# Passages between stages in program order with early products, and triangle matrices on ScalarE

## The chip, the cores and the metric

The kernel runs on one core of one Trainium2 chip. The core has TensorE for matrix products, VectorE, ScalarE and GpSimd for work on elements, each with a queue of its own that is worked off in order, and DMA queues for transfers (all weights come over SyncE's). Engines wait for one another by semaphores. The metric is the device time of one execution in microseconds (us); a value is the median of several runs.

## The reference

256 tokens with 1024 features pass through one network in float32. A root-mean-square norm stands in front of each part, and each part's result is added to `x`:

```
x = x + mixer(norm(x))            # window attention and gated linear attention
x = x + (silu(conv(h@Wa)) * (h@Wu)) @ Wo     with h = norm(x)     # FFN, causal conv over 3 tokens
x = x + pool_mixer(norm(x))       # causal means over 2, 4, 8, 16 tokens, then one product per group
x = x + (silu(h@Wg) * (h@Wu)) @ Wd           with h = norm(x)     # dense FFN
x = x + ssd(norm(x))              # state-space mixer, 32 heads of 64 in 8 groups, chunks of 128 tokens
x = x + top-2 of 8 experts(norm(x))
norm(x) = x / sqrt(mean(x*x) + 1e-6) * gain
```

In the state-space mixer each head has a decay `dtA` per token. Within a chunk the weight of token s in token l is exp of the sum of `dtA` over the tokens between them, for s up to l, times the inner product of two projected vectors; the result takes that matrix times the inputs, plus the state carried over from the chunk before.

## The kernel before

**Tiling.** The 256 tokens are two tiles of 128, t = 0 and 1. A row of 1024 features is two halves of 512, c = 0 and 1. Each float32 operand of a product is held as a high and a low part, and a product is done three times (high by high, high by low, low by high): `mm3`, L337 to L341, or, with the tokens as the moving side, one product of 2x256 columns and one of 256 (`sums`, L761, L770 and L771).

**Weights.** A piece is 1 MB, 128x2048. SyncE's queue fetches it into a ring of raw pieces; `piece` (L294) then splits it in two halves of 1024 columns: ScalarE copies the high part (`wh`, L391), VectorE subtracts it to get the low part (`wl`, L392). `wh` and `wl` have a ring of six halves each, so a seventh copy waits until TensorE is through with the first.

**A norm and its passage.** `norm_tile` (L368) squares the two halves on ScalarE (L373, with a sum per token), multiplies the second half by the gain on GpSimd (L374), and VectorE adds the two sums (L376) and makes the inverse root in eight small steps (`rsqrt`: `rs_x` L354, `rs_y` L358, then `rs_t` L361 and `rs_y` L365 three times). Then VectorE scales the first half (L378) and ScalarE the second (L379) into `xn`. `turn` transposes `xn` on TensorE (L404) and splits the result into `xT`, again a copy on ScalarE and a subtraction on VectorE. `Turned.tile` (L60) does this for one tile. For the FFN and the dense FFN it puts 11 dummy products (`keep_warm`, L62) in front of the second tile's transposes, and sets gates: the low part of the next weight piece is made by GpSimd, and the three pieces behind it are split only after the last `xT` split.

**What comes before a passage.** The mixer ends with `w_out` (two chunks of 512 columns, each with two pieces held, first tile 0, then tile 1), the FFNs with `down`: three pieces held, 36 products for tile 0 and then 36 for tile 1. `PoolMixer.tile` (L82) stands between the FFN and the dense FFN: its means are products with a band matrix (L99, and L101 for the first tile's tokens or the second's), then one product per group and `add_x` (L431).

**The state-space mixer.** `ssd` (L838) interleaves by a list of steps: `x0` to `x7` project and convolve a chunk of channels (products L756 to L758 into `acc`, convolution L802 and L805, gating L935 and L936), `z` chunks project the gate, and `c0` to `c7` are the cores, one for each group of four heads. A core makes, for each tile and for the high and low part of `dtA`, four triangle matrices side by side (`ua`, 128x512, L972): the upper triangle of ones times the decay of its row, on GpSimd. TensorE sums them (L974), ScalarE takes exp (`w`, L976), VectorE multiplies by the inner products (L977), and TensorE applies the result (L982). GpSimd also scales the inputs (`xd`, `xe`, `xs`, L952 to L955).

**What sets the order.** A list scheduler that runs the program in a model of the chip puts each engine's instructions in order. `in_order(begin)` (L1464) pins the order in which those since `begin` were written, on TensorE, VectorE and ScalarE, among themselves; instructions written later can still be put between them.

## Time and profile before

| | us |
|---|---|
| median of 3 runs | 1767.45 (1766.4 to 1769.3) |
| profiled execution | 1770.0 |
| its span | 1768.2 |

| engine | busy us | share of the span |
|---|---|---|
| TensorE (PE) | 1721.1 | 97% |
| VectorE (DVE) | 1495.5 | 85% |
| ScalarE (ACT) | 1245.7 | 70% |
| GpSimd (POOL) | 154.0 | 9% |

The stages follow one another: the mixer to 251, the FFN from 259 to 444, the pool mixer, the dense FFN from 465 to 649, the state-space mixer to 880, the router, and the experts from some 905 to 1740. A matmul's record is longer than the distance to the next, so TensorE's share of 97% is not a share of its peak; how dense the products are is read from the distances of their starts. Idle time of an engine counts only where another waits for it.

### The profile page before, as it was taken

How to read it: one execution, taken by the hardware profiler on the slowest of the kernel's cores; microseconds unless marked ns; L12 is line 12 of the kernel's file. 1: busy time of each engine (PE TensorE's matmuls, PEld its weight loads, DVE VectorE, ACT ScalarE, POOL GpSimd, SP SyncE). 2: the span in 40 equal slices, each digit the busy share in tenths (PEclk: the TensorE clock that was granted, in tenths of full speed). 3: DMA queues.
4: the chain of work that ended last, by engine and by line, in shares of the span. 5: the costliest groups of instructions: out<-in, count | busy, mean ns of one | idle time of the engine just before them, and what ended most of it. 6: DMA issues, size and time to landing. Idle time of an engine off the chain costs nothing.

```text
span 1768.2 us, 23830 instructions
## 1 busy us (share of the span) xinstructions
PE 1721.1 (97%) x8731; PEld 1420.7 (80%) x8731; DVE 1495.5 (85%) x1652; ACT 1245.7 (70%) x1412; POOL 154.0 (9%) x118
## 2 busy tenths in 40 slices
PE   8999989999999999999999999999999999999996
PEld 6878878888788879998878777777777787777775
DVE  7477668777766659997779999999999999999997
ACT  5564446655655546555468898888889888988895
POOL 1034010001100012572000000000000000000000
PEclk9999999999999999999989999999999999999999
DMA  8433455555455545425659999999999999999993
GB/s 288 167 120 123 143 183 211 185 188 188 143 188 188 188 150 204 143 97 179 253 187 373 420 421 421 420 418 420 405 402 420 421 420 415 421 420 410 421 420 157
DMA packets 72719, 501.31 MB, mean 284 GB/s; under 512 B 8322, under 2 KB 9346, under 8 KB 14355
## 3 DMA queue, kind: packets, MB, share of 16 engines
q1 hardware_dynamic: 72594, 499.71, 72.7%
q8 instruction: 71, 1.16, 0.3%
q14 instruction: 54, 0.43, 0.1%
HBM read 498.63 MB, written 1.05 MB: 283 GB/s over the span
## 4 chain that ended last, share of the span: by engine, by line
PE 55%; DVE 32%; issue 9%; ACT 2%; POOL 1%; DMA 0%; DVEq 0%; SPq 0%; ACTq 0%
DVE wl L313 23%; PE acc L339 7%; PE acc L340 7%; PE acc L341 7%; PE pr L770 5%; PE tp L770 5%; PE tp L771 2%; PE pr L771 2%; PE pr L339 2%; PE pr L340 2%; PE pr L341 2%; PE pr L1219 1%; PE pr L1218 1%; PE acc L516 1%; DVE wl L392 1%
## 5 line engine op out<-in xcount | busy, mean ns | idle before, releaser
L313 DVE TENSOR_TENSOR wl<-raw,wh 128x2048 fp32r<-128x2048 f32 x330 | 736.7, 2280 | 0.0
L311 ACT ACTIVATE wh<-raw 128x2048 fp32r<-128x2048 f32 x330 | 620.9, 1913 | 70.2 <-PE pr L341 38.8
L392 DVE TENSOR_TENSOR wl<-raw,wh 128x1024 fp32r<-128x1024 f32 (+2 forms) x248 | 308.2, 1255 | 112.7 <-ACT wh L391 109.8
L391 ACT ACTIVATE wh<-raw 128x1024 fp32r<-128x1024 f32 (+3 forms) x254 | 259.3, 1036 | 90.0 <-PE acc L341 60.1
L1219 PE MATMUL pr<-wl,xg 128*128 128x512 f32 x560 | 221.9, 396 | 5.5 <-DVE wl L313 5.5
L1218 PE MATMUL pr<-wh,xg 128*128 128x512 f32 x560 | 224.2, 400 | 0.0
L340 PE MATMUL pr<-wl,xg 128*128 128x512 f32 x336 | 135.8, 404 | 1.5 <-DVE wl L1462 1.5
L339 PE MATMUL pr<-wh,xg 128*128 128x512 f32 x336 | 136.6, 407 | 0.0
L341 PE MATMUL pr<-wh,xg 128*128 128x512 f32 x336 | 134.1, 399 | 0.0
L1219 PEld LDWEIGHTS pr<-wl,xg 128*128 128x128 f32 x560 | 105.3, 188 | 33.9 <-DVE wl L313 12.5
L770 PE MATMUL pr<-xT,wh 128*128 128x512 f32 x352 | 125.0, 398 | 2.0 <-DVE xT L392 2.0
L770 PE MATMUL tp<-xT,wh 128*128 128x512 f32 x352 | 124.9, 398 | 0.0
L1218 PEld LDWEIGHTS pr<-wh,xg 128*128 128x128 f32 x560 | 105.3, 188 | 22.2
L1219 PE MATMUL acc<-wl,hT 128*128 128x512 f32 x280 | 113.3, 405 | 1.6 <-DVE wl L313 0.4
L1218 PE MATMUL acc<-wh,hT 128*128 128x512 f32 x280 | 111.1, 397 | 0.7 <-DVE hT L392 0.7
L339 PE MATMUL acc<-wh,xT 128*128 128x512 f32 (+3 forms) x256 | 99.2, 389 | 1.6 <-ACT xT L391 0.9
L340 PE MATMUL acc<-wl,xT 128*128 128x512 f32 (+3 forms) x256 | 98.8, 387 | 0.0
L771 PE MATMUL tp<-xT,wl 128*128 128x256 f32 x352 | 98.6, 280 | 0.0
L771 PE MATMUL pr<-xT,wl 128*128 128x256 f32 x352 | 98.6, 280 | 0.0
L341 PE MATMUL acc<-wh,xT 128*128 128x512 f32 (+3 forms) x256 | 98.5, 387 | 0.1
L1536 POOL TENSOR_TENSOR raw<-x,raw 128x512 f32<-128x512 f32 x2 | 2.5, 1276 | 936.4 <-DVE x L431 936.4
L770 PEld LDWEIGHTS pr<-xT,wh 128*128 128x128 f32 x352 | 66.1, 188 | 18.4 <-DVE xT L392 2.4
(389 smaller groups left out, 3472.6 us busy)
## 6 DMA issues: line engine op xcount, KB each, us to landing
raw<-in_w_eg SPq DMA_DIRECT2D x110, 1024.0 KB, 10.6
raw<-in_w_ed SPq DMA_DIRECT2D x110, 1024.0 KB, 10.6
raw<-in_w_eu SPq DMA_DIRECT2D x110, 1024.0 KB, 10.8
raw<-in_w_ffn_in SPq DMA_DIRECT2D x22, 1024.0 KB, 4.9
raw<-in_w_dense_in SPq DMA_DIRECT2D x22, 1024.0 KB, 4.9
raw<-in_w_xbc SPq DMA_DIRECT2D x16, 1024.0 KB, 4.8
raw<-in_w_ffn_out SPq DMA_DIRECT2D x11, 1024.0 KB, 5.0
raw<-in_w_dense_out SPq DMA_DIRECT2D x11, 1024.0 KB, 4.9
```

The costliest lines, as they stand in the source:

```text
L311: self.nc.scalar.activation(ab[0], raw, AF.Copy)
L313: lambda: v.tensor_tensor(ab[1], raw, ab[0].bitcast(F32), op=OP.subtract)
L339: mm(ps, st[0], mv[0], start=start, stop=False)
L340: mm(ps, st[0], mv[1], start=False, stop=False)
L341: self.last_mm = mm(ps, st[1], mv[0], start=False, stop=stop)
L391: a = nc.scalar.activation(h, src, AF.Copy)
L392: b = v.tensor_tensor(l, src, h.bitcast(F32), op=OP.subtract)
L516: nc.tensor.matmul(ps[:, m], wt.cut(a, k * 256 + m * P, P), xT[b][:, k], start=(k == 0 and a == 0 and b == 0), stop=(k == KB - 1 and b == 1))
L770: nc.tensor.matmul(ps, wh, xT[2][:, k], start=k == 0, stop=False)
L771: nc.tensor.matmul(ps[:, 0], wl, xT[0][:, k], start=False, stop=k == KB - 1)
L1218: self.nc.tensor.matmul(ps, st, mv[0], start=start, stop=False)
L1219: self.nc.tensor.matmul(ps, st, mv[1], start=False, stop=stop)
```

## The change

**Norms.** `Normed` takes the place of `norm_tile`: `half(t, c)` squares one half as soon as its sum is there, with the factor 1/(2*1024) inside the square, and VectorE multiplies the first half by the gain; `scale(t)` makes the root in one VectorE step fewer (`rsqrt_of`), ScalarE scales the first half and VectorE makes the second. The dummy products of the passages and the gates are gone.

**Early piece.** `Lead` fetches and splits the first weight piece of the next stage during the passage, outside `piece`. `LeadSums` makes its products for one tile and half of the piece at a time: 8 products of 256 columns and 8 of 128, four times, so 64 products in place of 32 of 512 and 256 columns. `LeadRows` does the same for the mixer's first gate chunk (416 columns, four halves of 832).

**Program order.** `gemm_nat(then=)`, `down_last`, `ready`, `rest` and `both` write the passages out step by step, and `in_order` pins them.

**Triangle matrices.** Each `ua` is made by four ScalarE copies of 128x128 with a scale per partition, 128 in all, in place of one GpSimd product.

```diff
+    def half(self, t, c):
+        net, nc, xn = self.net, self.net.nc, self.xn
+        h = slice(c * 512, (c + 1) * 512)
+        nc.scalar.activation(xn[:, t, 512:], net.x[:, t, h], AF.Square, scale=(0.5 / D) ** 0.5,
+                             accum_out=self.ss[t][:, c:c + 1])
+        if c == 0:
+            nc.vector.tensor_tensor(xn[:, t, h], net.x[:, t, h], self.g[:, h], op=OP.mult)
+
+    def scale(self, t):
+        net, nc, xn = self.net, self.net.nc, self.xn
+        r = net.rsqrt_of(self.ss[t], 1e-6)
+        nc.scalar.activation(xn[:, t, :512], xn[:, t, :512], AF.Copy, scale=r)
+        nc.vector.scalar_tensor_tensor(xn[:, t, 512:], net.x[:, t, 512:], r, self.g[:, 512:], op0=OP.mult, op1=OP.mult)
...
+    def rest(self):
+
+        lead, n = self.lead, self.lead.n
+        lead.subtract(n // 2)
+        self.scale(1)
+        for u in range(n // 2 + 1, n):
+            lead.subtract(u)
+        for u in range(n // 2 + 1):
+            lead.products(0, u, self.xT)
+        self.turn(1)
+        for u in range(n // 2 + 1, n):
+            lead.products(0, u, self.xT)
+        for u in range(n):
+            lead.products(1, u, self.xT)
+
+    def both(self):
+
+        ps = [self.group(0, g) for g in range(2)]
+        self.group(0, 0, ps[0])
+        net, s = self.net, slice(0, P)
+        net.nc.scalar.activation(self.xT[0][:, 4:, s], ps[1], AF.Copy)
+        self.scale(1)
+        self.early = net.nc.vector.tensor_tensor(self.xT[1][:, 4:, s], ps[1], self.xT[0][:, 4:, s].bitcast(F32), op=OP.subtract),
+        self.lead.products(0, 0, self.xT)
+        self.turn(1)
+        self.lead.products(0, 1, self.xT)
+        for h in range(2):
+            self.lead.products(1, h, self.xT)
+
...
+    def fetch(self):
+        raws = [self.net.fetch(ap, self.w) for ap in self.aps]
+        w = self.w // 2
+        self.raw = [raw[:, h * w:(h + 1) * w] for raw in raws for h in range(2)]
+        self.n, self.high, self.low = len(self.raw), {}, {}
+
+    def copy(self, u):
+        self.high[u] = self.net.whp.tile([P, 1024], F32R, name="wh")[:, :self.w // 2]
+        self.net.nc.scalar.activation(self.high[u], self.raw[u], AF.Copy)
...
+    def products(self, t, h, xT):
+        net, mm = self.net, self.net.nc.tensor.matmul
+        if (t, h) == (0, 0):
+            self.ps = [net.pr((P, 2, T)) for _ in range(2)]
+        s = slice(t * P, (t + 1) * P)
+        for k in range(4 * h, 4 * h + 4):
+            for m in range(2):
+                c = slice(k % 4 * 256 + m * P, k % 4 * 256 + (m + 1) * P)
+                mm(self.ps[m][:, :, s], self.high[h][:, c], xT[2][:, k, :, s], start=k == 0, stop=False,
+                   skip_group_check=True)
+                mm(self.ps[m][:, 0, s], self.low[h][:, c], xT[0][:, k, s], start=False, stop=k == KB - 1,
+                   skip_group_check=True)
...
+    def rest(self):
+        net, N = self.net, self.N
+        N.lead.subtract(1)
+        self.scale(1)
+        out = self.mix(0)
+        ps = self.banks()
+        self.means(1, 0, ps)
+        for c in range(2):
+            net.add_x(0, c, out[c])
+            N.half(0, c)
+        self.means(1, 1, ps)
+        self.split(1, ps)
+        N.scale(0)
+        out = self.mix(1)
+        for c in range(2):
+            net.add_x(1, c, out[c])
+            N.half(1, c)
+        N.both()
+        self.ctx.close()
...
-            gate = self.gates.pop(0) if self.gates else ()
-            if None in gate:
-                v = self.nc.gpsimd
-            for ins in gate:
-                if ins is not None:
-                    st.enter_context(self.tc.issue_after(ins.ins))
-            fine = fine or self.wide is None or len(gate) > 0
+            fine = fine or self.wide is None
...
+    def rsqrt_of(self, ss, eps):
+
+        v = self.nc.vector
+        z = self.small.tile([P, 1], F32, name="rs_x")
+        t = self.small.tile([P, 1], F32, name="rs_t")
+        y = self.small.tile([P, 1], F32, name="rs_y")
+        v.tensor_scalar(z, ss[:, 0:1], ss[:, 1:2], 0.5 * eps, op0=OP.add, op1=OP.add)
+        v.tensor_scalar(y.bitcast(I32), z.bitcast(I32), -0.5, float(0x5F3759DF - 0x400000 - 0x80000000), op0=OP.mult, op1=OP.add)
+        for _ in range(3):
+            v.tensor_scalar(t, y, y, z, op0=OP.mult, op1=OP.mult)
+            v.scalar_tensor_tensor(y, t, -1.5, y, op0=OP.add, op1=OP.mult)
+        return y
...
+            if then is not None and p == np_ - hold:
+                then.fetch()
+                for h in range(2):
+                    then.lead.copy(h)
+                    then.lead.subtract(h)
...
             def end(t, c, ps):
+                if (t, c) == (0, 1):
+                    self.start = len(nc.cur_bb.bb.instructions)
                 self.add_x(t, c, ps)
-                if c:
-                    N.tile(t)
-
-            for c in range(2):
-                self.gemm_nat(mT, I["w_out"][c], KB, end, c, last=True)
+                N.half(t, c)
+                if (t, c) == (0, 1):
+                    N.scale(0)
+
+            self.gemm_nat(mT, I["w_out"][0], KB, end, 0, last=True)
+            self.gemm_nat(mT, I["w_out"][1], KB, end, 1, last=True, then=N)
+            N.both()
+            self.in_order(self.start)
...
+        begin = len(self.nc.cur_bb.bb.instructions)
+        for c in range(2):
+            self.add_x(0, c, accs[0][c])
+            N.half(0, c)
+        N.scale(0)
+        for c in range(2):
+            for j in range(len(aps)):
+                if (c, j) == (1, 1):
+                    N.ready()
+                sums(1, c, j)
+            self.add_x(1, c, accs[1][c])
+            N.half(1, c)
+        N.rest()
+        self.in_order(begin)
...
-            z_chunk(0)
+            for t in range(2):
+                gate_z(t, 0, N.lead.ps[t][:, :416])
...
                         ua = wk.tile([P, 4, P], F32R, name="ua")
-                        nc.gpsimd.tensor_tensor(ua, self.upper[:, None, :].to_broadcast([P, 4, P]),
-                                                bc(da[:, t, hs].bitcast(F32), P), op=OP.mult)
+                        for r in range(4):
+                            nc.scalar.activation(ua[:, r], self.upper, AF.Copy,
+                                                 scale=da[:, t, 4 * g + r:4 * g + r + 1].bitcast(F32))
                         nc.tensor.matmul(ps, laterr, ua, start=j == 0, stop=j == 1)
```

Three places show what the change does to the order. The first is VectorE around the first tile's norm in front of the FFN; `rs_x`, `rs_y`, `rs_t` are the steps of the inverse root, `wl<-raw,wh` the low half of a weight piece. Before:

```order
L376 TENSOR_TENSOR ss_2109<-ss 128x1
L354 TENSOR_SCALAR rs_x<-ss_2109 128x1
L358 TENSOR_SCALAR rs_y<-rs_x 128x1
L361 TENSOR_SCALAR rs_t<-rs_y,rs_x 128x1
L365 SCALAR_TENSOR_TENSOR rs_y<-rs_t,rs_y 128x1
L361 TENSOR_SCALAR rs_t<-rs_y,rs_x 128x1
L365 SCALAR_TENSOR_TENSOR rs_y<-rs_t,rs_y 128x1
L361 TENSOR_SCALAR rs_t<-rs_y,rs_x 128x1
L365 SCALAR_TENSOR_TENSOR rs_y<-rs_t,rs_y 128x1
L378 SCALAR_TENSOR_TENSOR xn<-x,rs_y,gbc 128x512
L431 TENSOR_TENSOR x<-x,acc 128x512
```
VectorE at the same place now:

```order
L527 TENSOR_SCALAR rs_y<-rs_x 128x1
L529 TENSOR_SCALAR rs_t<-rs_y,rs_x 128x1
L530 SCALAR_TENSOR_TENSOR rs_y<-rs_t,rs_y 128x1
L544 TENSOR_TENSOR wl<-raw,wh 128x1024
L529 TENSOR_SCALAR rs_t<-rs_y,rs_x 128x1
L544 TENSOR_TENSOR wl<-raw,wh 128x1024
L530 SCALAR_TENSOR_TENSOR rs_y<-rs_t,rs_y 128x1
L544 TENSOR_TENSOR wl<-raw,wh 128x1024
L529 TENSOR_SCALAR rs_t<-rs_y,rs_x 128x1
L544 TENSOR_TENSOR wl<-raw,wh 128x1024
L530 SCALAR_TENSOR_TENSOR rs_y<-rs_t,rs_y 128x1
L69 SCALAR_TENSOR_TENSOR xn<-x,rs_y,gbc 128x512
```
Four subtractions of weights, of the second and third piece of the FFN (L544; those of the early piece have L153), now stand between the steps of one root.

The second is ScalarE in the pool mixer's passage, from the second tile's first square to its scaling (`xn,ss<-x` is a square, `xn<-xn,rs_y` the scaling, `pT<-tp` the means). Before:

```order
L373 ACTIVATE xn,ss<-x 128x512
L379 ACTIVATE xn<-xn,rs_y 128x512
L391 ACTIVATE wh<-raw 128x1024
L373 ACTIVATE xn,ss<-x 128x512
L391 ACTIVATE pT<-tp 128x4x128 x2
L373 ACTIVATE xn,ss<-x 128x512
L379 ACTIVATE xn<-xn,rs_y 128x512
```
ScalarE at the same place now:

```order
L60 ACTIVATE xn,ss<-x 128x512
L543 ACTIVATE pT<-tp 128x4x128 x2
L149 ACTIVATE wh<-raw 128x1024 x2
L543 ACTIVATE wh<-raw 128x1024 x4
L60 ACTIVATE xn,ss<-x 128x512
L68 ACTIVATE xn<-xn,rs_y 128x512
```
Six copies of weights stand between the means' copies and the second tile's last square, four of them of the pieces behind the early one; before it was one copy, further ahead.

The third is ScalarE in the state-space mixer, from one `w` to the next but one (`cv`, `xbc` belong to the convolution, `wh` to weights, `Bn` to the core). Before:

```order
L976 ACTIVATE w<-tp 128x512
L391 ACTIVATE wh<-raw 128x1024
L935 ACTIVATE xbc_6515<-cv 128x256
L802 ACTIVATE cv<-acc,cols 128x256
L391 ACTIVATE wh<-raw 128x1024
L802 ACTIVATE cv<-acc,cols 128x256
L976 ACTIVATE w<-tp 128x512
```
ScalarE at the same place now:

```order
L1170 ACTIVATE w<-tp 128x512
L1166 ACTIVATE ua<-tri,dtAl 128x128 x4
L1156 ACTIVATE Bn<-tp 128x128
L543 ACTIVATE wh<-raw 128x1024
L1128 ACTIVATE xbc_6480<-cv 128x256
L543 ACTIVATE wh<-raw 128x1024
L1128 ACTIVATE xbc_6547<-cv 128x256
L1166 ACTIVATE ua<-tri,dtAh 128x128 x4
L1170 ACTIVATE w<-tp 128x512
```
Each row `ua` with x4 is four new copies; they stand between the convolutions, the exponentials and the weight splits.

## Rows read from the trace of the kernel before

**Rows 1.** TensorE's timeline, first passage: start us, us, engine line op out<-in xcount [idle<-releaser]

```profile
251.31 1.03 PE L404 MATMUL tp<-ident,xn 128*128 128x128 f32 x8
253.32 2.79 PE L335 MATMUL tp<-xT 128*128 128x512 f32 x11 [0.98 <-DVE xT L392]
...
258.90 0.50 PE L770 MATMUL pr<-xT,wh 128*128 128x512 f32 x1 [0.98 <-DVE xT L392]
...
264.65 0.40 PE L770 MATMUL tp<-xT,wh 128*128 128x512 f32 x1
```

**Rows 2.** TensorE's timeline, third passage

```profile
654.79 1.90 PE L404 MATMUL tp<-ident,xn 128*128 128x128 f32 x8 [2.18 <-DVE xn L378]
```

**Rows 3.** Windows: stretch, its us, then each engine's busy us (instructions), granted clock, DMA

```profile
core 0: us, PE busy (x) PEld busy (x) DVE busy (x) ACT busy (x) POOL busy (x), PEclk, DMA share, GB/s
654.80:658.20 3.40, 3.40 (x13) 2.91 (x14) 1.45 (x3) 2.08 (x4) 0.00 (x0) 0.51 0.07 14
690.00:760.00 70.00, 68.48 (x542) 65.97 (x541) 69.25 (x113) 40.86 (x78) 41.76 (x39) 1.00 0.37 126
760.00:850.00 90.00, 89.28 (x546) 81.06 (x545) 72.52 (x107) 49.33 (x88) 37.20 (x33) 1.00 0.50 179
```

**Rows 4.** The chain that ended last, mixer stage: start us, us, what

```profile
753.06 5.45 POOL ua L972 x4
```

**Rows 5.** VectorE's timeline in the mixer stage

```profile
694.86 1.26 DVE L936 SCALAR_TENSOR_TENSOR xbc<-xbc,cv 128x256 f32<-128x256 f32 x1
...
702.50 0.41 DVE L936 SCALAR_TENSOR_TENSOR xbc<-xbc,cv 128x256 f32<-128x256 f32 x1
```

**Rows 6.** Groups of VectorE, 690 to 850: xcount, busy us, mean ns, idle before

```profile
L936 DVE SCALAR_TENSOR_TENSOR xbc<-xbc,cv 128x256 f32<-128x256 f32 x27 | 18.1, 673 | 2.7 <-ACT xbc L935 2.7
```

**Rows 7.** ScalarE's timeline, first passage

```profile
246.85 0.63 ACT L373 ACTIVATE xn<-x 128x512 f32<-128x512 f32 x1 [4.04 <-DVE x L431]
...
250.13 0.72 ACT L379 ACTIVATE xn<-xn,rs_y 128x512 f32<-128x512 f32 x1 [2.55 <-DVE rs_y L365]
...
258.50 3.90 ACT L391 ACTIVATE wh<-raw 128x1024 fp32r<-128x1024 f32 x4
```

**Rows 8.** VectorE's timeline, first passage

```profile
248.18 0.15 DVE L354 TENSOR_SCALAR rs_x<-ss 128x1 f32<-128x1 f32 x1
...
250.07 0.75 DVE L378 SCALAR_TENSOR_TENSOR xn<-x,rs_y,gbc 128x512 f32<-128x512 f32 x1
...
259.59 3.50 DVE L392 TENSOR_TENSOR wl<-raw,wh 128x1024 fp32r<-128x1024 f32 x3
```

**Rows 9.** TensorE's timeline, second passage

```profile
447.53 0.28 PE L339 MATMUL pr<-wh,pT 128*128 128x256 f32 x1
447.65 0.28 PE L340 MATMUL pr<-wl,pT 128*128 128x256 f32 x1
...
470.26 0.39 PE L770 MATMUL tp<-xT,wh 128*128 128x512 f32 x1
```

**Rows 10.** VectorE's timeline, second passage

```profile
443.80 0.69 DVE L431 TENSOR_TENSOR x<-x,acc 128x512 f32<-128x512 f32 x1 [2.54 <-PE acc L341]
...
449.91 0.75 DVE L378 SCALAR_TENSOR_TENSOR xn<-x,rs_y,g 128x512 f32<-128x512 f32 x1
```

**Rows 11.** Groups of GpSimd, 660 to 880

```profile
L972 POOL TENSOR_TENSOR ua<-tri,dtAl 128x512 fp32r<-128x512 f32 x16 | 24.5, 1529 | 0.6 <-PE tp L974 0.4 <-DVE dtAl L392 0.2
L972 POOL TENSOR_TENSOR ua<-tri,dtAh 128x512 fp32r<-128x512 f32 x16 | 22.2, 1389 | 23.9 <-issue 19.1 <-PE tp L974 4.8
```

**Rows 12.** Groups of ScalarE, 690 to 850

```profile
L976 ACT ACTIVATE w<-tp 128x512 f32<-128x512 f32 x16 | 9.5, 592 | 7.5 <-PE tp L974 7.5
...
L963 ACT ACTIVATE Bn<-tp 128x128 f32<-128x128 f32 x8 | 2.2, 270 | 1.8 <-PE tp L960 1.8
```

**Rows 13.** Groups of TensorE, 690 to 760

```profile
L756 PE MATMUL acc<-xT,wh 128*128 128x256 f32 x136 | 39.3, 289 | 0.0
...
L974 PE MATMUL tp<-ua,laterr 128*128 128x512 f32 x18 | 7.1, 441 | 0.8 <-POOL ua L972 0.8
```

More of the change, by code (lines that the diff above doesn't have):

```diff
@@ new lines, with __init__, group, turn @@
+class Turned(Normed):
+    def __init__(self, net, gname, lead=None):
+        super().__init__(net, net.gain(gname), net.norm.tile([P, 2, D], F32, name="xn"))
+        self.xT, self.lead = net.pair(KB), lead and lead(net)
+    def fetch(self):
+        self.lead.fetch()
+    def group(self, t, g, turned=None):
+        net, nc = self.net, self.net.nc
+        s = slice(t * P, (t + 1) * P)
+        if turned is None:
+            turned = net.tp((P, 4, P))
+            for i in range(4):
+                nc.tensor.transpose(turned[:, i], self.xn[:, t, (4 * g + i) * P:(4 * g + i + 1) * P], net.ident)
+            return turned
+        last = net.split(turned, *[x[:, 4 * g:4 * g + 4, s] for x in self.xT[:2]])
+        if t == 0:
+            self.early = last
+    def turn(self, t):
+        for g in range(2):
+            self.group(t, g, self.group(t, g))
+    def ready(self):
+        self.turn(0)
+        self.lead.ready()
+    def rest(self):
[23 more added lines that the diff above has]
+            self.lead.products(1, h, self.xT)
@@ new lines, with products @@
+class LeadRows(Lead):
+    def products(self, t, u, xT):
+        net, w = self.net, self.w // 4
+        if u == 0:
+            if t == 0:
+                self.ps = []
+            self.ps.append(net.acc())
+        s = slice(t * P, (t + 1) * P)
+        for i in range(2):
+            k, c = 2 * u + i, slice(i * w, (i + 1) * w)
+            net.mm3(self.ps[t][:, :w], (xT[0][:, k, s], xT[1][:, k, s]), (self.high[u][:, c], self.low[u][:, c]),
+                    k == 0, k == KB - 1)
+class PoolMixer(Normed):
@@ L73, in __init__ @@
     def __init__(self, net, then):
[L74 removed]
+        self.then, self.N = then, None
         I = net.I
@@ L832, in ffn @@
             N = then()
-            self.down([w_out[i + j] for j in range(3)], hs[2 * i:], accs, False, self.add_x, then=N)
+            self.down_last([w_out[i + j] for j in range(3)], hs[2 * i:], accs, N)
         return N
```

144 lines of the change are left out of this document (78 added, 66 removed).

## The prediction

> **What bounds the kernel now.** I first read the time by stretch, then, at the places the change touches, the timeline of TensorE and behind it those of VectorE and ScalarE, and last the chain that ended last. Two kinds of place are touched. At the passages between stages TensorE stands and waits for a normalized row: before the FFN it fills part of the wait with 11 dummy matmuls, 253.32 to 256.11, and only at 258.90 does the first weight piece start; the second starts at 264.65 [rows 1]. Before the state-space mixer it waits 2.18 us, for VectorE [rows 2]. In the mixer TensorE is busy, but VectorE is at its limit too: 69.25 of 70 us from 690 to 760, and 72.52 of 90 after it, with ScalarE at 40.86 and 49.33 and GpSimd at 41.76 and 37.20 [rows 3]. There GpSimd's triangle matrices hold the chain too, 5.45 us on end for four of them at 753 [rows 4], and VectorE's operations with two inputs in SBUF are stretched while GpSimd runs: the gating of `xbc` takes 1.26 us at 694.86, with a triangle matrix beside it, and 0.41 at 702.50 [rows 5]; its mean over 27 is 0.673 [rows 6]. What lies behind the mixer and its router's norm is unchanged.
>
> The sum is made against the profiled execution of 1770.0 us (span 1768.2, and 1.8 around it), which lies 2.55 above the median of 1767.45; I carry the sum of differences over to the median.
>
> **First passage, mixer to FFN.** The order of the changed kernel decides it: between the steps of the first tile's inverse root, VectorE has the four subtractions of weight pieces 1 and 2 of the FFN. Each waits for ScalarE's high copy, and that for a free half in the ring of six. The ring is full by then (four halves of `w_out`, two of the early piece), so the copies follow the halves of `w_out` as the second tile's last products give them free; the last is free where the transposes start before, 251.3 [rows 1]. From there a copy, 0.98 (3.90 for four [rows 7]), a subtraction, 1.17 (3.50 for three [rows 8]), the last root step and the product with the gain, 0.16 and 0.75, and some 0.4 between engines: the first tile's row is ready at 254.9 to 255.2, where before it was ready at 250.8 (250.07 + 0.75 [rows 8]). The second tile's sum and square (0.6 and 0.8) stand before the copies of the transposed row, so the first copy and subtraction end at 257.9. The early products of half a piece for one tile are 16; their prices are 0.12 for 256 columns (447.53 to 447.65 [rows 9]) and about 0.11 for 128 (eight transposes in 1.03 [rows 1]), so 1.84 a group, and 7.36 for four groups against 5.75 for the piece whole (258.90 to 264.65 [rows 1]). The first group fits in the wait. The second tile's root chain (1.89 from 248.18 to 250.07, and 0.75 [rows 8]) ends at 260.3, its transposes at 261.4, and three groups at 266.9. Against 264.65 that is **+2.2 us**. Without the subtractions inside the chain all of it would lie 4 us earlier and be limited by the second tile's own sum at 251.3: some 263.9, or -0.7.
>
> **Second passage, FFN to pool mixer to dense FFN.** Here four copies stand on ScalarE before the second tile's last square, and four subtractions on VectorE before its root. Its last sum was started at 443.80 [rows 10]; eight mean products (0.9) now stand before it, 444.8. The two copies of the early piece end at 445.0, the four others at 448.9, the four subtractions at 451.7, root and product at 454.2 (1.89 + 0.75 from rows 8). Before, that row was ready at 450.66 (449.91 + 0.75 [rows 10]): 3.5 later. From there I walk the order: second half of the means 455.1; the copies of the means behind the square of the new sum, 456.7; first split 458.05; 24 products 460.95; transposes of the dense FFN's first tile 462.15; their copies behind both squares of the second tile, split 464.9; one early group; the second tile's row at 467.25, transposed 468.35; three early groups to 473.85. The second dense piece started at 470.26 [rows 9]: **+3.6 us**, and 0 if the row kept its old time.
>
> **Third passage, dense FFN to the state-space mixer.** Four copies of 832 and two of 1024 columns stand before the second tile's last square. Its row comes at 657.1 where its transposes started at 654.79 before [rows 2]; 18 of the first tile's 24 products are done in the wait. Two more weight splits stand before the second tile's own. I get **+1.2 us**, bounds -0.5 and +2.
>
> **The clock.** The dummies go and TensorE now stands still for 3.7 us in the first passage and 5.5 and 3 in the second. Where it waited 2.18 us before, it came back at a granted clock of 0.51 from 654.8 to 658.2 [rows 2, 3], the lower of the two levels, and its eight transposes took 1.90 where eight at the full clock took 1.03 [rows 1, 2]. In the first passage such a stretch, from 255.2 on, falls mostly into the wait for the second tile. In the second it would fall on the 24 products. Bounds 0 and +4; I take **+1.0**, near the lower end, since most of such stretches are covered by waits that remain.
>
> **The first norm** gets a product with the gain on VectorE inside the chain in place of GpSimd's: bounds 0 and +1.5, I take **+0.5** since TensorE waits for weights right after. **The router** has one VectorE step less in each of two chains: **-0.3**.
>
> **The triangle matrices.** GpSimd loses 16 of 1.529 and 16 of 1.389 us, 46.7 in all [rows 11]; ScalarE gets 128 of 128x128 with a scale per partition. The trace has no such row. A copy with a scale per partition takes 0.72 for 512 columns [rows 7]; 512 against 128 columns is 0.592 against 0.270 [rows 12], so 0.40 for one, and about 0.1 of that overlaps the next (a copy of 1024 is 0.98 of pitch): 0.30, 38 us in all. From the 0.270 row itself it would be 0.17 and 22 us. I take 0.30, the row with the same kind of scale. The Trainium skill ("ScalarE: Activation LUTs", What ACT_TABLE_LOAD costs) gives 186 ns plus 0.833 ns per column, 93 ns more for a pointer operand and 93 ns of overlap between neighbours: an estimate of 0.293 us, 37.5 in all. It speaks against the change, and agrees with the upper row.
>
> ScalarE then has 18 matrices in the first stretch (one for each product of 512 columns [rows 13]), 72 operations or 21.6 us, on top of 40.86: 62 of 70, in a queue that also feeds every weight split and convolution. VectorE gets time back: 27 gatings of 0.673 against 0.41 are 7 us by themselves, over the stage [rows 6], and GpSimd keeps about 2/5 of its work there. The Trainium skill ("SBUF — State Buffer", SBUF: two separate sides) states the reason as a lock: a VectorE operation with two SBUF inputs and a GpSimd operation exclude each other for the whole instruction. The pair of rows 5 agrees, 0.41 against 1.26; by that rule alone the relief would be the larger end of what follows. TensorE's own gaps bound the gain: in 690 to 760 its 542 products [rows 3] (three lines of 136 with 256 columns at 0.12, 18 with 512 [rows 13] at 0.23, the other 116 at 0.11) fill 66 of 70 us, so 4, and about as much again behind 760, where GpSimd still holds the chain [rows 4] and so few rows speak that I take the same: at most -9, as an estimate. On the other side, a ScalarE that is 90% full in order could cost as much as it gives, up to +4. The row nearest is ScalarE's load with its new work, 62 of 70: I take **-3.5**.
>
> **Sum**: 2.2 + 3.6 + 1.2 + 1.0 + 0.5 - 0.3 - 3.5 = +4.7, so 1774.7 for an execution like the profiled one, and 1772 for the median.
>
> **Rivals.**
> - *Mixer relief whole* (15%): ScalarE's queue keeps up, TensorE runs at its pitches: -9 in place of -3.5, 1766.7. For it: VectorE at 69.25 of 70. Against: ScalarE at 62 of 70.
> - *The splits ahead come early* (17%): ring halves and weights are there before the root chain reaches them, and the passages cost -0.5 in all, with 0.5 of clock: 1767.45 - 0.5 + 0.5 + 0.5 - 0.3 - 3.5 = 1764.1. Against it: the six halves are all held until the last products.
> - *Both* (8%): 1758.6. This is the one clearly faster.
> - *ScalarE's queue decides in the mixer* (10%): from the point at which a triangle operation takes more than 0.35 us (18 x 4 x 0.35 + 40.86 = 66 of 70), the products of the mixer wait for ScalarE and the weight splits queue behind it: +4 in place of -3.5, 1779.7.
> - *It does not do what it says* (5%): the passages' waits come out the same as before, 1767.
>
> The forecast has 45%, with its own range 1768 to 1777. About 0.2%, 3.5 us, is what a measurement of this kernel can tell from no change. Faster than 1763.9: both, half of the early splits, and the tails of the forecast and the relief, 0.23. Slower than 1771.0: most of the forecast, ScalarE's queue, 0.44. Within: 0.33. The range leaves out most of "both" and half of ScalarE's queue: 1760 to 1779.
>
> **What would show it.** In the changed profile: the first FFN piece after the early one starts 16 us after the last `w_out` product (13.5 before), and VectorE's subtractions stand between two root steps; TensorE's wait before the second half of the means is 5 us and more; GpSimd's share falls from 9% to about 6%; the gating of `xbc` has a mean near 0.5; ScalarE passes 60 of 70 in the mixer's first stretch. I am wrong if the triangle operations take 0.2 us or less, if the high copies are done before the root chain starts, or if the half clock falls on the products of the passages.

## Result and profile after

| | before | after |
|---|---|---|
| median of 4 runs, us | 1768.38 (1766.4 to 1769.4) | 1778.58 (1778.18 to 1778.85) |
| profiled execution, us | 1770.0 | 1778.49 |
| its span, us | 1768.2 | 1776.7 |

Before has one run more here than above. The changed kernel is slower by 10.2 us: ratio 1.0058, 95% interval 1.0046 to 1.007. The prediction had the direction, but a loss of less than half that size (1772). Its forecast's own range, 1768 to 1777, does not hold the time; the wider range, 1760 to 1779, does, by 0.4 us.

The first part of the page of after: the span, then each engine's busy us, its share and its instructions.

```profile
span 1776.7 us, 23967 instructions
PE 1721.1 (97%) x8773; PEld 1426.6 (80%) x8773; DVE 1488.0 (84%) x1656; ACT 1280.4 (72%) x1540; POOL 74.5 (4%) x70
```

TensorE is as busy as before to the tenth, and the kernel is 8.5 us longer: by shares of the whole span nothing has happened. So I cut both traces into stretches, each between the starts of two named instructions: the first `x` addition after `w_out`, after the FFN's `down` and after the dense FFN's `down`; the first `cv` of the state-space mixer; the first transpose of the router's norm; the first addition of the experts.

| stretch | before, us | after | forecast |
|---|---|---|---|
| start to the end of the first mixer | 235.19 | +1.33 | +0.5 |
| first passage and FFN | 200.23 | +3.16 | +2.2 and a part of the clock's +1.0 |
| second passage, pool mixer and dense FFN | 204.83 | +6.26 | +3.6 and a part of it |
| third passage | 30.12 | +2.26 | +1.2 and a part of it |
| state-space mixer | 204.40 | -3.95 | -3.5 |
| router and first experts | 229.01 | -0.91 | -0.3 |
| rest | 664.46 | +0.33 | 0 |

The three passages together lose 11.7 us where 8.0 were forecast. The seven terms sum to the 8.5 us by which the profiled executions differ; the medians differ by 1.7 us more, and which stretch holds that the two traces don't say. How far one execution can be trusted shows in the kernels below whose code in a stretch is the same: their first passages differ by up to 0.05 us, the second by 0.9, the third by 0.5, and the start by 3.6 (a part of that is a matter of the clock, see the first norm below).

**First passage.** VectorE's timeline of after, from a step of the first tile's root to its product with the gain:

```profile
251.03 0.27 DVE L529 TENSOR_SCALAR rs_t<-rs_y,rs_x 128x1 f32<-128x1 f32 x1
251.21 1.23 DVE L544 TENSOR_TENSOR wl<-raw,wh 128x1024 fp32r<-128x1024 f32 x1
252.35 0.15 DVE L530 SCALAR_TENSOR_TENSOR rs_y<-rs_t,rs_y 128x1 f32<-128x1 f32 x1
252.62 1.23 DVE L544 TENSOR_TENSOR wl<-raw,wh 128x1024 fp32r<-128x1024 f32 x1
253.76 0.27 DVE L529 TENSOR_SCALAR rs_t<-rs_y,rs_x 128x1 f32<-128x1 f32 x1
253.98 1.23 DVE L544 TENSOR_TENSOR wl<-raw,wh 128x1024 fp32r<-128x1024 f32 x1
255.12 0.15 DVE L530 SCALAR_TENSOR_TENSOR rs_y<-rs_t,rs_y 128x1 f32<-128x1 f32 x1
255.31 0.75 DVE L69 SCALAR_TENSOR_TENSOR xn<-x,rs_y,gbc 128x512 f32<-128x512 f32 x1
```

Root steps of 0.15 to 0.27 us stand apart by a subtraction of 1.23 each, and each subtraction waits for its copy. ScalarE's timeline of after shows what the copies wait for (in brackets the idle time before, and the releaser):

```profile
250.11 1.06 ACT L543 ACTIVATE wh<-raw 128x1024 fp32r<-128x1024 f32 x1 [0.26 <-PE acc L493]
251.52 1.06 ACT L543 ACTIVATE wh<-raw 128x1024 fp32r<-128x1024 f32 x1 [0.34 <-PE acc L493]
252.89 1.06 ACT L543 ACTIVATE wh<-raw 128x1024 fp32r<-128x1024 f32 x1 [0.31 <-PE acc L493]
```

It is `acc L493`, the second tile's last products of `w_out`, as forecast: the ring of six halves is full, and the first tile's root waits for the second tile's products, which it has nothing to do with. TensorE's timeline of after:

```profile
252.41 0.39 PE L493 MATMUL acc<-wh,xT 128*128 128x512 f32 x1
256.09 1.65 PE L90 MATMUL tp<-ident,xn 128*128 128x128 f32 x8 [3.29 <-ACT xn L68]
258.74 0.58 PE L175 MATMUL pr<-xT,wh 128*128 128x256 f32 x1 [1.00 <-DVE xT L544]
...
262.22 1.58 PE L90 MATMUL tp<-ident,xn 128*128 128x128 f32 x8
263.55 0.36 PE L175 MATMUL pr<-xT,wh 128*128 128x256 f32 x1
...
269.13 0.45 PE L932 MATMUL tp<-xT,wh 128*128 128x512 f32 x1
```

TensorE starts the first tile's transposes 3.7 us after the start of its last product; before, the two followed one another [rows 1]. The first early group, 16 products, takes 3.48 us (258.74 to 262.22), the other three 5.58 together (263.55 to 269.13), so 1.86 each.

**Second passage.** ScalarE's timeline of after, then VectorE's, in front of the second tile's row:

```profile
448.07 2.00 ACT L149 ACTIVATE wh<-raw 128x1024 fp32r<-128x1024 f32 x2
449.97 3.88 ACT L543 ACTIVATE wh<-raw 128x1024 fp32r<-128x1024 f32 x4
453.76 0.62 ACT L60 ACTIVATE xn<-x 128x512 f32<-128x512 f32 x1
```

```profile
452.08 4.62 DVE L544 TENSOR_TENSOR wl<-raw,wh 128x1024 fp32r<-128x1024 f32 x4
456.62 0.20 DVE L526 TENSOR_SCALAR rs_x<-ss 128x1 f32<-128x1 f32 x1
...
458.56 0.75 DVE L69 SCALAR_TENSOR_TENSOR xn<-x,rs_y,g 128x512 f32<-128x512 f32 x1
```

The sum that the square at 453.76 needs had been there since 451.1 (started at 450.34); the six copies stood ahead of it, and the four subtractions ahead of the root. TensorE, in the same passage of after, then waits 4.38 us:

```profile
459.34 3.78 PE L227 MATMUL tp<-band,xn 128*128 128x128 f32 x16 [4.38 <-ACT xn L68]
462.77 0.56 PE L491 MATMUL pr<-wh,pT 128*128 128x256 f32 x1
...
467.11 1.09 PE L90 MATMUL tp<-ident,xn 128*128 128x128 f32 x8 [0.30 <-ACT xn L68]
471.08 0.39 PE L175 MATMUL pr<-xT,wh 128*128 128x256 f32 x1 [2.88 <-DVE xT L544]
...
474.21 1.40 PE L90 MATMUL tp<-ident,xn 128*128 128x128 f32 x8
...
480.94 0.45 PE L932 MATMUL tp<-xT,wh 128*128 128x512 f32 x1
```

The second dense piece starts at 480.94; the same place before is 470.26 [rows 9], and 4.49 of the 10.68 are brought along from ahead of the passage.

**Third passage.** ScalarE's timeline of after, up to the second tile's last square:

```profile
658.77 1.68 ACT L149 ACTIVATE wh<-raw 128x832 fp32r<-128x832 f32 x2
660.47 1.28 ACT L1089 ACT_TABLE_LOAD   x1
...
661.90 1.67 ACT L149 ACTIVATE wh<-raw 128x832 fp32r<-128x832 f32 x2
663.48 1.99 ACT L543 ACTIVATE wh<-raw 128x1024 fp32r<-128x1024 f32 x2
665.37 0.61 ACT L60 ACTIVATE xn<-x 128x512 f32<-128x512 f32 x1
```

The table load and its `ea` (an exponential of 32 columns), 1.43 us from start to next start, stand in this chain now; in the trace of before they came at 650.78, behind the second tile's squares. The forecast had not counted them.

**Clock and mixer.** Windows of after, columns as in [rows 3]: 8.3 us of the first passage, 7.6 of the second, and the two stretches of the mixer.

```profile
core 0: us, PE busy (x) PEld busy (x) DVE busy (x) ACT busy (x) POOL busy (x), PEclk, DMA share, GB/s
255.20:263.50 8.30, 6.41 (x31) 6.01 (x32) 5.04 (x15) 3.31 (x7) 0.00 (x0) 0.59 0.64 237
459.30:466.90 7.60, 7.47 (x40) 7.21 (x40) 5.42 (x15) 3.10 (x7) 0.00 (x0) 0.65 0.28 112
690.00:760.00 70.00, 70.00 (x573) 69.20 (x573) 61.06 (x108) 54.59 (x124) 13.17 (x19) 1.00 0.43 147
760.00:850.00 90.00, 89.93 (x571) 81.79 (x571) 73.45 (x124) 71.01 (x165) 17.07 (x23) 1.00 0.36 123
```

The first two windows reach past it: cut to the 6.7 us from 256.5 and from 457.9, each has a granted clock of 0.50, the lower level (1.2 GHz). TensorE's work behind both waits falls into it. Before, the same passages (251.2 to 268 and 444 to 472) were granted 1.00 throughout. In the mixer TensorE's record has no gap left (68.48 of 70 before [rows 3]); VectorE is down from 69.25 to 61.06 and ScalarE up from 40.86 to 54.59.

Groups of after: VectorE's gating, 690 to 850, and ScalarE's triangle matrices, 660 to 880 (xcount, busy us, mean ns).

```profile
L1129 DVE SCALAR_TENSOR_TENSOR xbc<-xbc,cv 128x256 f32<-128x256 f32 x31 | 14.5, 472 | 2.9 <-ACT xbc L1128 2.9
...
L1166 ACT ACTIVATE ua<-tri,dtAh 128x128 fp32r<-128x128 f32 x64 | 20.8, 394 | 4.3 <-PE tp L1168 4.3
L1166 ACT ACTIVATE ua<-tri,dtAl 128x128 fp32r<-128x128 f32 x64 | 20.4, 396 | 0.0
```

The gating of `xbc` is down from 673 ns [rows 6] to 472.

### The profile page after: what moved, and what is told of

It is laid out like the page before. It is cut to its first block, busy times and chain, and to the rows that moved or that the text cites. A ratio compares the mean times of both kernels' runs of the same rounds, so it can differ in the third digit from the quotient of the medians.

```text
span 1776.7 us, 23967 instructions
## 1 busy us (share of the span) xinstructions
PE 1721.1 (97%) x8773; PEld 1426.6 (80%) x8773; DVE 1488.0 (84%) x1656; ACT 1280.4 (72%) x1540; POOL 74.5 (4%) x70
## 4 chain that ended last, share of the span: by engine, by line
PE 59%; DVE 29%; issue 9%; ACT 2%; DMA 0%; DVEq 0%; SPq 0%; ACTq 0%
DVE wl L465 23%; PE acc L491 7%; PE acc L492 7%; PE acc L493 7%; PE tp L932 5%; PE pr L932 4%; PE tp L933 2%; PE pr L933 2%; PE pr L491 2%; PE pr L493 2%; PE pr L492 2%; PE acc L919 2%; PE acc L920 2%; PE acc L918 2%; PE pr L1413 1%
## 5 line engine op out<-in xcount | busy, mean ns | idle before, releaser
L544 DVE TENSOR_TENSOR wl<-raw,wh 128x1024 fp32r<-128x1024 f32 (+2 forms) x246 | 301.8, 1238 | 121.5 <-ACT wh L543 118.7
L543 ACT ACTIVATE wh<-raw 128x1024 fp32r<-128x1024 f32 (+2 forms) x246 | 252.3, 1038 | 91.8 <-PE acc L493 55.7
L493 PE MATMUL pr<-wh,xg 128*128 128x512 f32 x336 | 133.8, 398 | 0.0
L1413 PEld LDWEIGHTS pr<-wl,xg 128*128 128x128 f32 x560 | 105.4, 188 | 33.9 <-DVE wl L465 12.5
L932 PE MATMUL pr<-xT,wh 128*128 128x512 f32 x320 | 113.5, 397 | 0.0
L493 PE MATMUL acc<-wh,xT 128*128 128x512 f32 (+3 forms) x256 | 98.9, 388 | 0.0
L933 PE MATMUL pr<-xT,wl 128*128 128x256 f32 x320 | 89.6, 280 | 0.0
L492 PEld LDWEIGHTS pr<-wl,xg 128*128 128x128 f32 x336 | 63.7, 189 | 19.6 <-DVE wl L465 3.8
L932 PEld LDWEIGHTS tp<-xT,wh 128*128 128x128 f32 x352 | 66.1, 188 | 16.2
```

Source lines behind the costliest of these rows:

```text
L492: mm(ps, st[0], mv[1], start=False, stop=False)
L493: self.last_mm = mm(ps, st[1], mv[0], start=False, stop=stop)
L543: a = nc.scalar.activation(h, src, AF.Copy)
L544: b = v.tensor_tensor(l, src, h.bitcast(F32), op=OP.subtract)
L932: nc.tensor.matmul(ps, wh, xT[2][:, k], start=k == 0, stop=False)
L933: nc.tensor.matmul(ps[:, 0], wl, xT[0][:, k], start=False, stop=k == KB - 1)
```

## The experiments

My theory (A): the loss is in the passages, mostly the weight copies and subtractions of the pieces behind the early one, which the scheduler puts inside the norms' chains, and to a smaller part the lower clock behind the waits; the triangle matrices alone are a gain. The rival (B): the early half-piece products and the new program order cost the time by themselves, so that holding the splits back changes little. Each run is compared with runs of before of its own round, whose medians are 1767.9 to 1768.9. Lengths of stretches are differences to before unless said otherwise, and "the passages" are the second to fourth row of the table above.

### The splits held back

Gates like those that the change took away come back, and the passage to the state-space mixer, which had none, gets them too: the pieces behind the early one (three in the passages to the FFN and the dense FFN, two in that to the state-space mixer) are split only after the passage's last `xT` split. All else is as in after.

```diff
@@ Turned, at the end of rest() and of both()
+        self.net.gates = [self.last] * 2
...
+        net.gates = [self.last] * 3
@@ piece
+            for ins in self.gates.pop(0) if self.gates else ():
+                st.enter_context(self.tc.issue_after(ins.ins))
```

> The changed kernel, but the splits of the three weight pieces behind the early one are let go only after the last split of the transposed rows, in all three passages (two pieces in the third). Theory A (weight splits placed inside the passages' chains delay the rows; the forecast's reason): the second FFN piece starts some 3 to 4 us earlier, the second dense piece 5 to 6 earlier in all, the third passage another 1 earlier; about -8 us against the changed kernel, so some 1770, within 3 us of the kernel before. Rival B (the early products in halves and the lost dummies are what costs, the splits are hidden by TensorE's own waits): less than 2 us of the 10 come back, 1776 or more.

Measured: 1767.3 us, ratio to before 0.9995 (0.9985 to 1.0005), 11.3 below after. The passages are -0.12, +2.47 and +0.09. VectorE's timeline of this run, the first tile's root in the first passage:

```profile
246.99 0.21 DVE L531 TENSOR_SCALAR rs_x<-ss 128x1 f32<-128x1 f32 x1 [0.85 <-ACT xn L60]
...
248.93 0.75 DVE L69 SCALAR_TENSOR_TENSOR xn<-x,rs_y,gbc 128x512 f32<-128x512 f32 x1
```

The root's steps follow one another again, 1.94 us from the first to the product with the gain, where after takes 6.38 (248.93 to 255.31). TensorE's timeline, first passage:

```profile
250.69 1.03 PE L90 MATMUL tp<-ident,xn 128*128 128x128 f32 x8
253.66 0.39 PE L178 MATMUL pr<-xT,wh 128*128 128x256 f32 x1 [1.93 <-DVE xT L549]
...
256.24 1.97 PE L90 MATMUL tp<-ident,xn 128*128 128x128 f32 x8 [0.41 <-ACT xn L68]
```

The transposes follow the last product without a wait again. The three passages give back 9.2 of 11.7 us: B falls, A holds, and the cause is shown, not only argued. It gave back more than A expected; the waits that shrink are also those that the lower clock follows, and the start of this execution is 1.95 us shorter than after's with the same code, 1.6 of it by the clock (see the first norm below).

### Dummy products in the waits, the splits left as they are

Products that nothing reads fill TensorE's waits: 14 and 5 in the first passage, 18 and 11 in the second, 15 in the third.

```diff
+    def fill(self, n, w):
+        ps = self.acc()
+        for i in range(n):
+            self.nc.tensor.matmul(ps, w[:, :P], w[:, :512], start=True, stop=True)
```

> The changed kernel with dummy products of 512 columns in TensorE's waits (14 before the first transposes and 5 before the early products in the first passage, 18 before the second half of the means and 11 before the early products in the second, 15 before the second tile's transposes in the third), nothing else changed. Theory A (half the excess over the forecast is the clock): the granted clock stays at its upper level in the passages, 0.9 us come back in the first passage, 2 to 3 in the second, 1 in the third: -4 us, 1774.5. Rival B (waits set the end of each passage, the clock only stretches what is covered): within 1 us of the changed kernel, or slower where a dummy stands in the way.

Measured: 1774.39 us, ratio 1.0036 (1.0022 to 1.0051), 4.2 below after. That is A's number, but not where A put it (0.9, 2 to 3 and 1): against after the passages are shorter by 1.19, 0.57 and 0.18 (in the second, the dense FFN's second tile is transposed 1.17 us earlier); the windows from 250 to 264 and from 450 to 475 are granted 1.00. So some 2 us of the 11.7 are the clock alone, with the waits where they are. The rest of the median's 4.2 is not in the passages of the trace; its start stretch is 3.6 shorter than after's, with the same code.

### Triangle matrices alone

The kernel before with only the last hunk of the diff: four ScalarE copies in place of each GpSimd product.

> The kernel before with only the triangle matrices made by ScalarE, 128 copies of 128x128. Theory A (VectorE is relieved of GpSimd, ScalarE keeps up): the state-space mixer is 3.5 us shorter, 1765 for 1768.4; VectorE's gating of xbc has a mean of 0.45 to 0.5 us. Rival B (ScalarE's queue takes the place): 0 to +4 us.

Measured: 1765.17 us, ratio 0.9983 (0.9973 to 0.9992), so -2.9 us, as A expected; the passages keep their length within the spread given above (-0.04, +0.86, -0.39) and the mixer is -4.19. The mixer's gain is the triangle matrices' own, and it doesn't depend on the rest of the change.

### Both remedies

The gates, with dummies fitted to the waits that remain: 8 in the first passage, 4 and 12 in the second, 7 in the third.

```diff
+        net.fill(4, N.lead.high[0])
         out = self.mix(1)
...
-            N.both()
+            N.both(8)
```

> The changed kernel with the gated splits of the earlier run, and dummy products of 512 columns sized to the waits that this left: 8 and 12 before the early products of the first and second passage, 4 before the second group products of the pool mixer, 7 before the second tile's transposes of the third. Theory A (after the splits, what is left of the passages' loss is the lower clock on the early products): the clock stays up, 1 us comes back in the first passage, 2 in the second, 0.7 in the third: 1763.5, below the kernel before by more than 0.2%. Rival B (the early products in halves wait for rows, not for the clock): 1766 to 1768, as with the gates alone.

Measured: 1762.12 us, ratio 0.9967 (0.9953 to 0.9981), near A's 1763.5 and below B's 1766. The passages are -1.88, +1.18 and -1.51, and the granted clock is 1.00 from 250 to 264 and from 430 to 475. With the splits out of the way the dummies are worth 4.7 us in the passages (+2.44 with the gates alone, -2.21 here, summed over the three), more than the 2 with the splits in them. I read this as TensorE's pace deciding more of a passage once the chain of rows is short; no run isolates it. With both, the change's passages are 2.2 us shorter than those of before.

### The first piece whole

With the gates; the early piece's products are made as before, 32 of 512 and 256 columns, after both tiles' rows. The question, on which A and B of this run and the next stand, is now whether the early products help: A has them neutral, B has them save time.

```diff
-        for k in range(4 * h, 4 * h + 4):
-            for m in range(2):
...
+        if (t, h) != (1, 1):
+            return
...
+                mm(self.ps[m], self.high[k // 4][:, c], xT[2][:, k], start=k == 0, stop=False)
+                mm(self.ps[m][:, 0], self.low[k // 4][:, c], xT[0][:, k], start=False, stop=k == KB - 1)
```

> The changed kernel with the gated splits, but the early piece of the FFN and of the dense FFN is multiplied whole, 32 products after both tiles' rows are there, in place of 64 in four groups of which one comes before the second tile's row. Theory A (the group that is hidden in the wait is worth 1.84 us a passage, the halving costs 1.75): within 0.7 us of the gated kernel, 1767. Rival B (the early group is a real gain): 2 us or more slower, 1769 to 1771.

Measured: 1770.85 us, ratio 1.0013 (1.0003 to 1.0022): A's number missed, B's held. TensorE's timeline of this run:

```profile
254.75 1.97 PE L90 MATMUL tp<-ident,xn 128*128 128x128 f32 x8 [4.50 <-ACT xn L68]
257.28 0.79 PE L178 MATMUL pr<-xT,wh 128*128 128x512 f32 x1 [0.56 <-DVE xT L547]
```

Without the early products the wait is 4.50 us in place of 1.93 and 0.41, the transposes behind it take 1.97, and the piece takes 7.18 us (to 264.46) where before it took 5.75 [rows 1]. The passages are +1.86, +4.60 and +1.31, 5.3 us more in sum than with the halves. So the early products save time; whether by themselves or by keeping the clock up, this run doesn't say.

### The first piece whole, full clock

The run before with 19, 4 and 23, and 7 dummies, so that TensorE has its full clock in all three passages.

> The kernel with gated splits and the early piece multiplied whole (the earlier run), now with dummy products in the waits: 19 before the second tile's transposes of the first passage, 23 in the second, 4 before the second group products, 7 in the third passage. Theory A (what made the whole piece dear was the lower clock that a longer wait brings, 7.34 and 8.48 us for products that take 5.75; the hidden early group is worth no more than the halving costs): the first passage is 0.5 to 1 us shorter than with halves and dummies, the second within 1 us of it; 1761 to 1764, like the run with halves and dummies. Rival B (the early group is a gain at either clock): 3 us or more above that run, 1765 or more.

Measured: 1765.36 us, ratio 0.9984 (0.9974 to 0.9993): 3.2 above the halves with dummies (the two intervals overlap by a little), where A had 1761 to 1764 and B at least 1765. The passages are -0.01, +2.35 and -1.49, against -1.88, +1.18 and -1.51: 3.05 us, close to the medians' 3.2. TensorE's timeline of this run, the first passage:

```profile
255.21 1.29 PE L90 MATMUL tp<-ident,xn 128*128 128x128 f32 x8 [0.17 <-ACT xn L68]
257.28 0.50 PE L180 MATMUL pr<-xT,wh 128*128 128x512 f32 x1 [0.78 <-DVE xT L555]
...
263.03 0.40 PE L943 MATMUL tp<-xT,wh 128*128 128x512 f32 x1
```

and of the run with halves and dummies:

```profile
254.76 1.29 PE L90 MATMUL tp<-ident,xn 128*128 128x128 f32 x8 [0.52 <-ACT xn L68]
255.80 0.36 PE L180 MATMUL pr<-xT,wh 128*128 128x256 f32 x1
...
261.38 0.45 PE L945 MATMUL tp<-xT,wh 128*128 128x512 f32 x1
```

From the second tile's transposes to the second piece it is 7.82 us whole and 6.62 in halves, at the same pace: the halves have a group of the first tile's to work on while the second tile's `xT` is split (the 0.78), and only three groups left in place of four. That is 1.2 of the 1.87 in this stretch; the other 0.7 builds up over the next 35 us of the FFN, 0.1 to 0.2 us per piece and with no wait of TensorE over 0.25 us, and its cause is open. So the early products are a gain of some 3 us, and B holds at the full clock as well.

### Half of the triangle matrices

The kernel before, with the 16 matrices of the high part made by ScalarE and the 16 of the low part left on GpSimd.

```diff
+                        if j:
+                            nc.gpsimd.tensor_tensor(ua, self.upper[:, None, :].to_broadcast([P, 4, P]),
+                                                    bc(da[:, t, hs].bitcast(F32), P), op=OP.mult)
+                        else:
+                            for r in range(4):
+                                nc.scalar.activation(ua[:, r], self.upper, AF.Copy,
```

> The kernel before with the triangle matrices of the high part of the decay made by ScalarE (64 copies of 128x128) and those of the low part left to GpSimd. Theory A (the gain comes from taking GpSimd off VectorE's second port and off the chain, in proportion): about half of what all 128 copies gave, 1766.7 for 1765.2 and 1768.1. Rival B (ScalarE's load is what limits the gain): as good as or better than all 128, 1765 or less.

Measured: 1763.64 us, ratio 0.9974 (0.9962 to 0.9985), where A's simple halving gave 1766.7 and B 1765 or less: B's number held. Mixer -5.34 against -4.19 with all 32 on ScalarE, router -2.18 against +0.34. The run's window, and its group on VectorE (690 to 850):

```profile
690.00:760.00 70.00, 70.00 (x564) 68.58 (x563) 66.02 (x115) 52.96 (x118) 31.00 (x35) 1.00 0.38 132
```

```profile
L936 DVE SCALAR_TENSOR_TENSOR xbc<-xbc,cv 128x256 f32<-128x256 f32 x27 | 14.6, 552 | 0.0
```

VectorE gets less relief (66.02 of 70, where all on ScalarE gave 60.30; gatings of 552 ns in place of 480) and the stage is shorter all the same. So more relief of VectorE does not by itself make the stage shorter. The load that fell is ScalarE's, 52.96 against 58.84 in this window; that it is what limits the full version fits, but is not shown, since TensorE's record has no gap in either window. The medians are 1.5 us apart with intervals that overlap, and of the 3.7 us that the two traces differ by in mixer and router, 2.5 lie in the router, where the clock differs too (see the account below).

### Best version

Both remedies, with half of the triangle matrices on GpSimd.

> Gated splits, halves and dummies as in the run at 1762.1, and only the high part's triangle matrices on ScalarE, the low part's on GpSimd. Theory A (the two are independent, the half gives 1.5 more in the mixer than all 128): 1760.5. Rival B (the mixer's gain depends on how the scheduler happens to interleave it): anywhere from 1760 to 1766, with the mixer's stretch not shorter than 200.7 us.

Measured: 1760.42 us, ratio 0.9954 (0.9937 to 0.997): 8.5 us below before and 18 below after. A's number was 1760.5, but its reason, 1.5 us more in the mixer than with all 128 copies, is not what the trace shows: the passages are -1.89, +0.42 and -1.49, the mixer -4.33 (-5.34 with half alone, -3.71 with all 128 and both remedies), the router -2.48 (-0.35). Most of what half adds here stands in the router.

## Why the prediction came out as it did

**Right: the mechanism of the passages.** The likeliest case held, with its cause: the first tile's root waits for the subtractions, these for the copies, and these for the ring (254.9 to 255.2 was forecast for the first row, though the terms named, 0.98, 1.17, 0.16, 0.75 and 0.4 from 251.3, sum to 254.8; 256.06 less the 1.33 that the trace is late by then is 254.7). The rival "the splits ahead come early" would have had to show root steps without gaps. The run with the gates shows that this order is worth 9.2 of the 11.7 us. The other side of that step, -0.7 for a first passage without the subtractions in the chain, lies between the -0.12 of that run and the -1.88 of the one with dummies too. The second piece starts 16.7 us after the last `w_out` product, with 16 forecast; TensorE's wait in front of the means is 4.38 us and not 5 and more.

**The range: luck.** The measured time lies above the forecast's own range. The wider one holds it because its upper part was meant for the rival "ScalarE's queue decides", and that rival did not come.

**Mis-sized: the clock, +1.0.** It is about 2 us with the waits as they are (dummies alone) and 4.7 with the splits held back. The step that failed is the sentence that the half clock "falls mostly into the wait for the second tile". In the first passage the first early group was to fit in the wait at 1.84 us; it took 3.48, and the second tile's transposes stood behind it: +0.96 over the +2.2, and the dummies gave back 1.19. My own row [rows 2] had shown that a wait of 2.18 us is followed by eight transposes at 1.90; I should have carried that pace through each step behind a longer wait, instead of one number for three passages. By the prediction's own signs it is wrong here: the half clock does fall on the products of the passages, on the first early group in the first and on the means and the products behind them in the second.

**Mis-sized: the second passage, +3.6 against +6.26.** By the dummies' run the clock is some 1.2 of the 2.66 that were missed, up to the second tile's transposes (the whole stretch gave back only 0.57). The 1.5 left is the chain of rows, also at the full clock: the second tile's row was ready 0.6 later than walked (copies and subtractions took what was reckoned, but began 0.5 later, behind the eight mean products: priced at 0.9, these take 1.81, 445.49 to 447.30, since each stands in the trace as two instructions, 16 rows), and the steps between the means and the last row took some 0.8 us more than walked. A part of that is a wait that the walk left out: the dense FFN's first transposes, at 467.11, wait for their own root, which VectorE takes up at 464.39, behind the means' second split, where the walk had them follow the 24 products.

**Mis-sized: the third passage, +1.2 against +2.26.** The row was forecast at 657.1, so at 667.85 with the 10.75 of delay by then; it came at 668.8. The table load and `ea`, 1.43 us, now ahead of the second tile's last square, cover that.

**Right: the mixer, -3.5 against -3.95** (-4.19 alone). ScalarE's price was right: 0.40 for one was forecast and 0.394 and 0.396 are measured, and four `dtAl` copies end 1.27 us after the first one's start, 0.29 from one to the next, with 0.30 forecast. The Trainium skill ("ScalarE: Activation LUTs", What ACT_TABLE_LOAD costs) gave the estimate of 0.293; the trace agrees. `xbc` was forecast near 0.5 and is 0.472. ScalarE did not pass 60 of 70 in the first stretch, 54.59; the stage starts 13 us later there, so the window holds another part of it. In the kernel with the triangle matrices alone, 2.3 us earlier, it is 58.84. GpSimd's share is 4%, not 6%: it lost its part of the norms too, which the 6% left out; with the triangle matrices alone it is 6%. That the gain stops at about 4 of the 9 us that TensorE's gaps allowed was put down to ScalarE's load; the run with half of the matrices fits that and does not show it.

**The rivals.** "ScalarE's queue decides" was to begin at 0.35 us per copy; at 0.29 it stayed out, and the mixer gained. "Mixer relief whole", -9, was not reached in any run; the most is -5.34, with half of the matrices. "Both", 1758.6, was not reached; with gates and dummies the change comes to 1762.12.

**Router, -0.3 against -0.91.** This stretch also holds the first experts' pieces, and it moves between -2.5 and +0.3 in the runs; both lowest values belong to the kernels with half of the triangle matrices on GpSimd. The ten traces sort by the clock: the mean granted clock of the stretch's first 45 us is 0.81 in the two longest (before, and +0.34 with the triangle matrices alone), 0.85 in the six between (-0.32 to -1.02, after among them) and 0.89 in the two shortest (-2.18 and -2.48). So the length of this stretch goes with the clock, and the VectorE step that was forecast cannot be read from it; why the clock falls for less time in some kernels is not isolated.

**First norm, +0.5, not measurable.** The start stretch is 236.29 in the best version and 233.09 in that with both remedies, with the same code. Half of that spread is the clock: in front of a group of transposes in the mixer (of `sgb`, at 226 to 229) TensorE waits 1.02 us in all ten traces; in before, after and the best version the next 3.3 us have a granted clock of 0.50 and it is 7.8 us to the first `x` addition, in the other seven the clock stays at 1.00 and it is 6.2. The seven kernels with the new norm have a mean of 234.3, the three with the old one 233.7. That is the forecast's size, but no evidence for it. It also limits what the table of stretches can say of after's +1.33.

## What to carry to other kernels

When code pins an order for a critical chain, look at what a scheduler can still put between the pinned steps: here work for the next stage, waiting on a full buffer ring, entered the chain of a tile that had no part in that wait, and one dependency per piece that held it back was worth more than what the mixer and the router gained. Price every step behind a wait of TensorE at the pace that the trace shows behind such waits, not at the pace of a running stretch. And where a load is moved off one engine, try half too: in two pairs of kernels half was 1.5 and 1.7 us faster than all in the medians, though with intervals that overlap.

## What the runs showed of the hardware

Waits of 1 to 2 us can be followed by TensorE's lower clock, and the same wait need not be. In the run with the gates the first tile's products start at full pace behind a wait of 1.93 us (granted 1.00 up to 255.4), but the second tile's eight transposes, after another 0.41, take 1.97 (granted 0.50 from 255.5 to 258.8). The wait of 1.02 us in the first mixer is followed by a granted clock of 0.50 in three of ten traces and of 1.00 in seven. Behind 4.38 us, 16 rows of means take 3.78 us where 16 without a wait ahead take 2.05. The rows show only what came before each; what decides it was not tested. And filling such waits with products that nothing reads, 31 of 512 columns in all, took 5.2 us off the median (1767.3 to 1762.12, each with its own runs of before), in a kernel of 1760.
